# Sample attention in visits of three cache tiles, tokens stored by parity, in a one-core decoder layer

## The chip, the cores and the metric

The kernel is one program on one core of a Trainium2 chip. The metric is the device time of one execution in microseconds (us); the time of a kernel is the median of its runs. The profile and the trace describe one further execution. In them PE is TensorE's matmul stream, PEld its weight loads, DVE is VectorE, ACT is ScalarE, POOL is GpSimd, and SP is the engine whose queue issues nearly all DMAs.

## What is computed

One decoder layer for 256 prompt tokens and 8 x 4 = 32 sample tokens together (288 columns, D = 2048, all in float32). Cut to what matters:

```python
z = x @ w_in                      # h, Bg, Cg, q, k, v, g_a, g_b
ya = Bg * causal_conv3(Cg * h)
# q, k, v: 3 groups (dilation 1, 4, 16) x 4 heads of 128; token t sees t - dil*i, i = 0..128
yb = attention(q, k, v)           # softmax over all groups of a head together
mixed = sigmoid(g_a) * (ya @ w_branch_a) + sigmoid(g_b) * (yb @ w_branch_b)
x1 = LN1(ALPHA * x + mixed @ w_out)
a, b = split(x1 @ w_up);  a = causal_conv3(a)
y = LN2(ALPHA * x1 + (silu(a) * b) @ w_down)
```

The prompt attends to itself only; the sample tokens also attend to a cache of old keys and values. The windows of cache rows, the last rows of both convolutions and the new keys and values are outputs too.

## The kernel before

**The products.** All weights stream once from HBM in blocks of 128 output features, up to 1 MB each. `prepare` (L162) issues a block's load on SP into one of three `wst` buffers, and `half_block` (L135) splits it, half by half, into a rounded part `whi` (ACT, L138) and the rest `wlo` (DVE, L139). `product` (L187) then runs `mms` (L202): per 128 input features three fp32r matmuls of 288 columns (L208 hi x hi, L209 hi x lo, L210 lo x hi), 48 for a full block, 36 for a block of the last third of the FFN. The activations are split likewise (`split`, L213). A token tensor is read as two halves of 144 tokens, one column from each in turn; the layer's input `xh`, `xl` lies with a pitch of HX = 160 elements between the halves, all others with 144. So the two columns of a pair in PSUM belong to tokens t and t + 144.

**The order of the products.** 12 blocks for q, 24 for k and v, 48 for the convolution mixer, 32 for gate a and `w_branch_a`, 32 for gate b and `w_branch_b`, 16 for `w_out` with LayerNorm 1 (class `Norm`, L614), then three parts of the FFN: `w_up` blocks and 16 `w_down` blocks each. The program is written in that order, and a scheduler of the framework orders each engine's instructions by dependences and its own estimate of time; `behind` and `in_a_row` add ordering edges by hand.

**Prompt attention** (L320) of head j begins when its k and v are there, and is cut by `yield` into three pieces which `prompt_step` puts behind later products: the scores (L326: for query blocks 0 and 1 of 128 tokens, 3 groups each, against 128 or 256 keys; 1152 columns of plain f32 matmuls), the softmax (DVE, ACT), then transposes of v (L346) and of the weights (L354: 9), and the weighted sums (L362: 9 matmuls of 128 columns). Distances and masks lie in `m_dist`.

**Sample attention** (`sample_steps`, L406) goes through the 18 tiles (1 MB) of cached keys, does a softmax, and goes through the 18 tiles of cached values. A *visit* takes the tiles in SBUF, two of them (two buffers `cache`): for each batch 4 matmuls, one per head, each in its own 32 columns of the PE array, with queries (or weights) that a mask has put to zero outside the batch (`by_batch`, L379, one DVE product of 1024 columns per group). L421 are the key visits, L474 the value visits, 9 of each. After a visit `fetch_two` (L389) issues two loads (L395) and the two stores of the tiles into the output windows (L396), all on SP. Visits are spread evenly from the first k block on: each product adds 20 to a count and each 101 of it call for a step. L438 holds the scores of the new keys, L485 the share of the new values, as matmul groups of their own.

**Elsewhere.** `gated` (L555), `conv_in`, `pieces` and `from_psum` move between halves and token order in three instructions per tensor. In the last FFN part POOL subtracts the mean estimate from each chunk of `dd` (L785) and adds up sums for LayerNorm 2 (L639, L640). The tail (`finish_out`, L673) normalises and stores y.

Of the kernel before, what the change touches and what calls it, by code (L numbers as in the profile page):

```python
# [17 lines left out]
P = 128  # L18
D = 2048
KD = D // P  # L20
SEQ = 256
# [4 lines left out]

H = T // 2
HG = H + 1
HX = 160
# [13 lines left out]
SW = NG * P + NG * NS  # L43
SLOPE = [[float(np.float32(2.0 ** (-8.0 * (g * NH + j + 1) / (NG * NH)))) for j in range(NH)] for g in range(NG)]
# [6 lines left out]
C_M0 = C_TM + NT  # L51
C_M1 = C_M0 + NG * P
# [16 lines left out]


N_STEP = N_CT + 2
N_STEP_BLOCKS = 2 * NG * NH + 5 * KD - 3
# [11 lines left out]
def layer_kernel(ctx: ExitStack, tc: tile.TileContext, ins, outs):  # L84
# [25 lines left out]

    def att(cols=512):
        return sb(ps, [P, cols], "att", bufs=2)
# [8 lines left out]
    spent = [0]  # L121
# [12 lines left out]

    def half_block(st, k0, n):  # L135
        hi = sb(wp, [P, HK, P], "whi", F32R, bufs=4)
        lo = sb(wp, [P, HK, P], "wlo", F32R, bufs=4)
        act.copy(hi[:, :n, :], st[:, k0 : k0 + n, :])  # L138
        dve.tensor_tensor(lo[:, :n, :], st[:, k0 : k0 + n, :], f32(hi[:, :n, :]), ALU.subtract)  # L139
        return hi, lo, n  # L140
# [46 lines left out]
    def product(x):  # L187

        w = w_ready.pop(0)
        if not w_ready:  # L190
            prepare()
        if steps_on[0]:
            spent[0] += N_STEP
            while spent[0] >= N_STEP_BLOCKS:
                spent[0] -= N_STEP_BLOCKS
                next(steps, None)
        o = acc(x[0].shape[-1])
        mms(o, w, x)
        prompt_step()
        return o.rearrange("p a h -> p h a")  # L200
# [36 lines left out]
    w_two_lo = [sb(wk, [P, 2, HK, P], "cache", F32R, bufs=2) for _ in range(2)]  # L237
# [46 lines left out]
    cst = sb(big, [P, C_M0], "cst")  # L284

    pa = sb(big, [P, KD * T], "yal")
    m_dist = pa[:, : C_W - C_M0]
    pa_at = [C_W - C_M0]

# [5 lines left out]
    s_two = [pa_take(NG * 2 * P) for _ in range(2)]  # L295
    xs_flat = xs.rearrange("p k t -> p (k t)")
    q_all = xs_flat[:, : NH * NG * T].rearrange("p (j g t) -> p j g t", j=NH, g=NG)
    sT_flat = [xs_flat[:, NH * NG * T + c * NG * P : NH * NG * T + (c + 1) * NG * P] for c in range(3)]
    sT_three = [t.rearrange("p (g q) -> p g q", g=NG) for t in sT_flat]
# [14 lines left out]

    def in_a_row(row):

        for before, i in zip(row, row[1:]):
            behind(i, before)

    def prompt_attention(j, qT, kT, vT):  # L320

        blocks = [(qb, g, P * (qb + 1)) for qb in range(2) for g in range(NG)]
        s3 = att(NG * P), att(2 * 2 * P), sb(ps, [P, 2 * P], "acc")
        p_at = [(s3[0], g * P) for g in range(NG)] + [(s3[1], 0), (s3[1], 2 * P), (s3[2], 0)]
        in_a_row([last_mm[0]] + [
            pe.matmul(t[:, c : c + nk], qT[:, g, qb * P : (qb + 1) * P], kT[:, g, :nk], start=True, stop=True)  # L326
            for (t, c), (qb, g, nk) in zip(p_at, blocks)
        ])
        s = [s_two[qb][:, : NG * P * (qb + 1)].rearrange("p (g k) -> p g k", g=NG) for qb in range(2)]
        for (t, c), (qb, g, nk) in zip(p_at, blocks):  # L330
            c0 = qb * NG * P + g * nk
            dve.scalar_tensor_tensor(
                s[qb][:, g, :], m_dist[:, c0 : c0 + nk], -SLOPE[g][j] / SCALE, t[:, c : c + nk], ALU.mult, ALU.add
            )
        for qb in range(2):
            st = sb(wk, [P, 4], "st", bufs=4)
            dve.reduce_max(st[:, 0:1], s[qb], AX.XY)
# [8 lines left out]
            pe.transpose(pv[kb][:, g * P : (g + 1) * P], vT[:, g, kb * P : (kb + 1) * P], ident)  # L346
# [4 lines left out]
        pairs = ((0, 0), (1, 0), (1, 1))  # L351
        pt = [att(NG * P), att(NG * P), sb(ps, [P, NG * P], "acc")]
        in_a_row(row + [
            pe.transpose(t[:, g * P : (g + 1) * P], s[qb][:, g, kb * P : (kb + 1) * P], ident)  # L354
            for t, (qb, kb) in zip(pt, pairs) for g in range(NG)
        ])
        for sT, t in zip(sT_three, pt):
            act.copy(sT, t.rearrange("p (g q) -> p g q", g=NG))
# [4 lines left out]
                po[:, qb * P : (qb + 1) * P], v[:, kb, g], sT[:, g],  # L363
                start=kb == 0 and g == 0, stop=kb == qb and g == NG - 1,
            )
            for sT, (qb, kb) in zip(sT_three, pairs) for g in range(NG)
        ])
        act.copy(oT, po)
        split(ybh[:, j, :SEQ], ybl[:, j, :SEQ], oT)


    bmask = cst[:, C_BM : C_BM + NB * NS].rearrange("p (b r) -> p b r", b=NB)
    tmask = cst[:, C_TM : C_TM + NT]

    sw = sb(wk, [P, NH * NB * NS + 1152], "sw", bufs=1)
    sw_m = sw[:, : NH * NB * NS].rearrange("p (j b r) -> p j b r", j=NH, b=NB)
    sw2 = sw[:, NH * NB * NS :]

    def by_batch(src):  # L379

        m = sw_m
        shape = [P, NH, NB, NS]
        dve.tensor_tensor(m, src.unsqueeze(2).broadcast_to(shape), bmask.unsqueeze(1).broadcast_to(shape), ALU.mult)
        return m
# [21 lines left out]
    def sample_steps():  # L406
        fetch_two()
        yield
        row = []
        s = sw2[:, :SW]  # L410
        sbias = cst[:, C_SB : C_SB + SW]
        for g in range(NG):
            qm = by_batch(q_s[:, g])
            cols = P if g == 0 else NT * P
            p = sb(ps, [P, cols], "long", bufs=1)
            for b in range(NB):
                if g > 0 or b % 4 == 0:
                    c = cache_tiles.pop(0)
                o = (b % 4) * NH * P if g == 0 else 0
                for j in range(NH):  # L420
                    row.append(pe.matmul(  # L421
                        p[j * NS : (j + 1) * NS], qm[:, j, b, :], c[:, o + j * cols : o + (j + 1) * cols],
                        start=b == 0, stop=b == NB - 1,
                    ))
                if b == NB - 1 or (g > 0 and b % 2 == 1):
                    in_a_row(row)
                    row = []
                    fetch_two()
                    yield
# [5 lines left out]
        pn = sb(ps, [P, NG * NS], "long", bufs=1)  # L435
        for j in range(NH):
            for g in range(NG):
                pe.matmul(  # L438
                    pn[j * NS : (j + 1) * NS, g * NS : (g + 1) * NS], q_s[:, g, j, :], k_s[:, g, j, :],
                    start=True, stop=True,  # L440
                )
        dve.tensor_tensor(s[:, NG * P :], pn, sbias[:, NG * P :], ALU.add)
        st = sb(wk, [P, 4], "st", bufs=4)
        dve.reduce_max(st[:, 0:1], s, AX.X)
        dve.tensor_scalar_mul(st[:, 1:2], st[:, 0:1], -SCALE)
        act.activation(s, s, AF.Exp, bias=st[:, 1:2], scale=SCALE, accum_out=st[:, 2:3])
        dve.reciprocal(st[:, 3:4], st[:, 2:3])
        dve.tensor_scalar_mul(s, s, st[:, 3:4])
        pt = att()
        for g in range(NG):  # L450
            pe.transpose(pt[:, g * P : (g + 1) * P], s[:, g * P : (g + 1) * P], ident)
        pt2 = att()
        pe.transpose(pt2[: NG * NS, :P], s[:, NG * P :], ident)
        sT = sw2[:, : NG * P].rearrange("p (g r) -> p g r", g=NG)
        act.copy(sT, pt[:, : NG * P].rearrange("p (g r) -> p g r", g=NG))
        sTn = sw2[: NG * NS, NG * P : NG * P + P]
        act.copy(sTn, pt2[: NG * NS, :P])
        vn = sw2[: NG * NS, NG * P + P : NG * P + P + NH * P].rearrange("p (j d) -> p j d", j=NH)
        pv = att()
        for j in range(NH):  # L460
            pe.transpose(pv[: NG * NS, j * P : (j + 1) * P], v_s[:, j].rearrange("p g r -> p (g r)"), ident)
        act.copy(vn, pv[: NG * NS].rearrange("p (j d) -> p j d", j=NH))
        o_sb = sw2[:, NG * P + P + NH * P : NG * P + 2 * P + NH * P]
        for g in range(NG):
            sm = by_batch(sT[:, g].rearrange("p (j r) -> p j r", j=NH))
            cols = P if g == 0 else NT * P
            if g < 2:
                p = sb(ps, [P, cols], "long", bufs=1)
            for b in range(NB):
                if g > 0 or b % 4 == 0:  # L470
                    c = cache_tiles.pop(0)
                o = (b % 4) * NH * P if g == 0 else 0
                for j in range(NH):
                    row.append(pe.matmul(  # L474
# [502 lines left out]
```

## Time and profile before

| | |
|---|---|
| median of 3 runs | 1762.09 us (1761.49 to 1762.12) |
| the profiled execution | 1763.11 us, span 1761.3 us |
| granted TensorE clock, mean | 0.997 of full speed |
| busy share: PE, DVE, ACT, POOL | 99%, 57%, 45%, 14% |
| HBM traffic over the span | 275 GB/s |

The span is the part of an execution that the trace covers; the profiled execution was 1.8 us longer than its span and 1.0 us longer than the median. A busy PE need not be PE at its peak: the time between the starts of two matmuls tells the pace.

### The profile page before, as it was taken

The numbers are of one execution on the slowest core, as the hardware profiler recorded it, in microseconds if no ns is written. First come the engines' busy times: TensorE is split into PE (matmuls) and PEld (weight loads), VectorE is DVE, ScalarE is ACT, GpSimd is POOL, SyncE is SP. The second block draws the span as 40 slices with busy tenths as digits, with TensorE's granted clock in tenths as the row PEclk, the third lists the DMA queues.
The fourth block names the chain that finished last, engine by engine and source line by source line (L and its number), as shares of the span: only waits on it lengthen the run. The fifth ranks groups of instructions, "written<-read, shape, count | busy, mean of one in ns | idle before, by whom it ended". The sixth has DMA issues, their size and how long they took to land.

```text
span 1761.3 us, 33600 instructions
## 1 busy us (share of the span) xinstructions
PE 1743.9 (99%) x14269; PEld 1714.4 (97%) x14269; DVE 1008.2 (57%) x1322; ACT 798.4 (45%) x1174; POOL 254.8 (14%) x403
## 2 busy tenths in 40 slices
PE   9999999999999999999999999999999999999996
PEld 9999999999999999999999999999999999999996
DVE  5444455545555444455588888774555554555554
ACT  5444444333434333344445656553454443345444
POOL 0000000000000000001155233310011110011174
PEclk9999999999999999999999999999999999999998
DMA  8477787787787887466766566656565656666662
GB/s 325 173 288 264 271 299 297 265 324 297 271 333 285 304 312 269 150 241 252 269 259 220 210 241 226 229 219 236 219 236 219 236 217 238 217 238 217 223 212 105
DMA packets 60919, 436.25 MB, mean 248 GB/s; under 512 B 7265, under 2 KB 8929, under 8 KB 16865
## 3 DMA queue, kind: packets, MB, share of 16 engines
q1 hardware_dynamic: 59040, 429.40, 65.9%
q10 hardware_dynamic: 1728, 4.72, 0.7%
q8 instruction: 111, 1.82, 0.4%
q14 instruction: 40, 0.32, 0.0%
HBM read 389.89 MB, written 94.53 MB: 275 GB/s over the span
## 4 chain that ended last, share of the span: by engine, by line
PE 96%; POOL 1%; ACT 1%; DVE 1%; issue 0%; DMA 0%; ACTq 0%; DVEq 0%
PE acc L208 31%; PE acc L210 31%; PE acc L209 31%; PE acc L276 1%; PE long L421 1%; PE long L474 1%; POOL dd L785 1%; PE att L362 0%; PE att L326 0%; ACT whi L138 0%; POOL qk_s L549 0%; ACT xh L214 0%; ACT yah L708 0%; DVE dd L684 0%; DMA yah<-in_x 0%
## 5 line engine op out<-in xcount | busy, mean ns | idle before, releaser
L139 DVE TENSOR_TENSOR wlo<-wst,whi 128x1024 fp32r<-128x1024 f32 (+1 forms) x578 | 706.9, 1224 | 617.3 <-ACT whi L138 613.2
L138 ACT CAST whi<-wst 128x1024 fp32r<-128x1024 f32 (+1 forms) x578 | 590.0, 1022 | 871.2 <-PE acc L209 767.7
L208 PE MATMUL acc<-xh,whi 128*128 128x288 f32 (+1 forms) x3216 | 923.0, 287 | 0.0
L210 PE MATMUL acc<-xh,wlo 128*128 128x288 f32 (+1 forms) x3216 | 920.5, 286 | 0.0
L209 PE MATMUL acc<-xl,whi 128*128 128x288 f32 (+1 forms) x3216 | 920.4, 286 | 0.0
L208 PEld LDWEIGHTS acc<-xh,whi 128*128 128x128 f32 x3216 | 607.8, 189 | 7.9 <-ACT h L569 2.5
L210 PEld LDWEIGHTS acc<-xh,wlo 128*128 128x128 f32 x3216 | 607.8, 189 | 0.8 <-issue 0.8
L209 PEld LDWEIGHTS acc<-xl,whi 128*128 128x128 f32 x3216 | 607.9, 189 | 0.3 <-issue 0.2
L208 PE MATMUL acc<-yah,whi 128*128 128x288 f32 x1216 | 348.0, 286 | 0.3 <-ACT yah L214 0.3
L210 PE MATMUL acc<-yah,wlo 128*128 128x288 f32 x1216 | 347.7, 286 | 0.6 <-DVE wlo L139 0.6
L209 PE MATMUL acc<-yal,whi 128*128 128x288 f32 x1216 | 347.6, 286 | 0.0
L208 PEld LDWEIGHTS acc<-yah,whi 128*128 128x128 f32 x1216 | 229.7, 189 | 3.1 <-ACT h L591 2.5
L210 PEld LDWEIGHTS acc<-yah,wlo 128*128 128x128 f32 x1216 | 229.8, 189 | 0.8 <-DVE wlo L139 0.8
L209 PEld LDWEIGHTS acc<-yal,whi 128*128 128x128 f32 x1216 | 229.8, 189 | 0.0
L549 POOL COPY qk_s<-u 128x2 f32<-128x2 f32 x44 | 41.5, 943 | 565.7 <-ACT u L758 441.1
L535 DVE SCALAR_TENSOR_TENSOR cy<-u,prm,cy 128x304 f32<-128x304 f32 x120 | 71.1, 593 | 3.4 <-ACT cy L533 0.7
L606 POOL TENSOR_TENSOR ya<-ya,dd 128x288 f32<-128x288 f32 x16 | 13.6, 851 | 306.0 <-DVE ya L605 306.0
L560 DVE TENSOR_TENSOR ya<-cy,acc 128x144 f32<-128x144 f32 x132 | 25.6, 250 | 33.6 <-PE acc L210 33.6
L549 POOL COPY cm<-u 128x2 f32<-128x2 f32 x16 | 3.0, 185 | 254.3 <-DVE u L574 254.3
L214 ACT CAST yah<-ya 128x288 fp32r<-128x288 f32 x76 | 32.7, 430 | 13.8 <-POOL ya L606 8.3
L214 DVE TENSOR_TENSOR yal<-ya,yah 128x288 fp32r<-128x288 f32 x76 | 34.9, 460 | 1.3 <-ACT yah L214 1.2
L639 POOL TENSOR_TENSOR cache<-cache,dd 128x288 f32<-128x288 f32 x29 | 28.0, 964 | 49.0 <-DVE dd L724 33.5
(179 smaller groups left out, 852.8 us busy)
## 6 DMA issues: line engine op xcount, KB each, us to landing
wst<-in_w_in SPq DMA_DIRECT2D x113, 1024.0 KB, 6.0
wst<-in_w_up SPq DMA_DIRECT2D x88, 1024.0 KB, 4.8
wst<-in_w_down SPq DMA_DIRECT2D x32, 1024.0 KB, 4.8
cache<-in_ck SPq DMA_DIRECT2D x18, 1024.0 KB, 6.4
out_o_ck<-cache SPq DMA_DIRECT2D x18, 1024.0 KB, 9.1
cache<-in_cv SPq DMA_DIRECT2D x18, 1024.0 KB, 6.3
out_o_cv<-cache SPq DMA_DIRECT2D x18, 1024.0 KB, 9.8
wst<-in_w_a SPq DMA_DIRECT2D x16, 1024.0 KB, 4.8
```

What stands on the lines that cost most here:

```text
L138: act.copy(hi[:, :n, :], st[:, k0 : k0 + n, :])
L139: dve.tensor_tensor(lo[:, :n, :], st[:, k0 : k0 + n, :], f32(hi[:, :n, :]), ALU.subtract)
L208: pe.matmul(out, hi[:, c, :], xh_k, start=k == 0, stop=False)
L209: pe.matmul(out, hi[:, c, :], xl_k, start=False, stop=False)
L210: last_mm[0] = pe.matmul(out, lo[:, c, :], xh_k, start=False, stop=k == nk - 1)
L214: return act.copy(hi, src), dve.tensor_tensor(lo, src, f32(hi), ALU.subtract)
L276: i = pe.matmul(o[b], first_w(term == 2, b, k), xk, start=k == 0 and term == 0, stop=k == KD - 1 and term == 2)
L421: row.append(pe.matmul(p[j * NS : (j + 1) * NS], qm[:, j, b, :], c[:, o + j * cols : o + (j + 1) * cols], start=b == 0, stop=b == NB - 1,))
L535: dve.scalar_tensor_tensor(y, u[:, i : i + YW], prm[:, w0 + i : w0 + i + 1], y, ALU.mult, ALU.add)
L549: pool.tensor_copy(dst[:, 0:2], u[:, SEQ : SEQ + 2])
L560: dve.tensor_tensor(a, b, c, ALU.mult)
L639: pool.tensor_tensor(self.s1, self.s1, d, ALU.add)
```

## The change

1. **Tokens by parity.** The two halves of a token tensor now hold the even and the odd tokens, so that a pair of PSUM columns is a pair of neighbours. `split` of the input reads x with a step of two; `conv_in`'s callers and `gated` write and read token order with a step of two, in two instructions where there were three (in part 0 of the FFN `gated` takes three where it took two). HX falls from 160 to 145.
2. **Prompt attention.** The query blocks are the even and the odd tokens. Dilations 4 and 16 keep the parity, so groups 1 and 2 need 128 keys per block and only group 0 needs 256: 1024 columns of score matmuls per head, 8 transposes of weights, 8 weighted sums.
3. **Sample attention.** Three `cache` buffers, and visits of three tiles, one each 8 products from the eighth q block on: 6 for keys and 6 for values. Each product calls `fetch`, which issues one load or one store. `by_batch` is called per batch, two products ahead of the visit. The new keys' scores and the new values' share ride in a visit. Accumulators lie partly in `att` buffers. Scratch moves into the `dd` buffer, and the mask array shrinks.
4. **Order.** Ordering edges put the re-split of x behind the splits of gated activations and weights (after part 0), and each subtraction of the mean on POOL behind the sums of three chunks earlier (last part).

The core of the diff:

```diff
-HX = 160
+HX = 145
+MW = (2 + NG - 1) * P
+N_VISIT = 3
+APART = 8
...
     def product(x):
         if steps_on[0]:
-            spent[0] += N_STEP
-            while spent[0] >= N_STEP_BLOCKS:
-                spent[0] -= N_STEP_BLOCKS
-                next(steps, None)
+            next(steps, None)
...
-        splits.append(split(xh[:, k, :, :H], xl[:, k, :, :H], h3(xs[:, k])))
+        splits.append(split(xh[:, k, :, :H], xl[:, k, :, :H], xs[:, k].rearrange("p k (a h) -> p k h a", h=2)))
...
     def prompt_attention(j, qT, kT, vT):
+        q4 = h3(qT)[:, :, :, :P]
+        k4, v4 = (t[:, :, :SEQ].rearrange("p g (a h) -> p g h a", h=2) for t in (kT, vT))
+        for qb in range(2):
+            row += [
+                pe.matmul(s3[qb][:, : 2 * P], q4[:, 0, qb], kT[:, 0, :SEQ], start=True, stop=True)
+            ] + [
+                pe.matmul(s3[qb][:, (1 + g) * P : (2 + g) * P], q4[:, g, qb], k4[:, g, qb], start=True, stop=True)
+                for g in range(1, NG)
+            ]
...
-    def fetch_two():
-        for _ in range(2):
+    def fetch():
+        if to_store:
+            sp.dma_start(*to_store.pop())
+        elif len(cache_tiles) < N_VISIT:
             which, n = next(cache_left, (None, 0))
             if which:
-                t = sb(wk, [P, 2048], "cache", bufs=2)
+                t = sb(wk, [P, 2048], "cache", bufs=3)
                 behind(sp.dma_start(t, ins[which][n]), w_load[0])
-                sp.dma_start(outs["o_" + which][n], t)
+                to_store.append((outs["o_" + which][n], t))
                 cache_tiles.append(t)
...
+        for values in range(2):
+            p = [None] * NG
+            for first in range(0, N_CT, N_VISIT):
+                here = held[first : first + N_VISIT]
+                for n in range(APART):
+                    fetch()
+                    if values and first == 0 and n == 3:
+                        transposed()
+                    if n == APART - 2:
+                        at = 0
+                        for g, batches in here:
+                            for b in batches:
+                                by_batch(at, sT[:, g].rearrange(...) if values else q_s[:, g], b)
+                                at += 1
+                    yield
...
+                        for j in range(NH):
+                            row.append(pe.matmul(
+                                p[g][j * NS : (j + 1) * NS], sw_m[:, len(row) // NH, j], c[:, o + j * cols : o + (j + 1) * cols],
...
+                if values and 0 in rest_of:
+                    row += [ ... the share of the new values, into p[0] ... ]
+                elif not values and NG - 1 in rest_of:
+                    pn = att(NG * NS)
+                    row += [ ... the scores of the new keys, into pn ... ]
+                in_a_row(row)
...
         for i in range(KD):
             o = product((h3(gh), h3(gl)))
             if part == 0:
-                split(x[0][:, i], x[1][:, i], h2(dd[:, i]))
+                for i_x, *before in zip(split(x[0][:, i], x[1][:, i], h2(dd[:, i])), last_split, w_split):
+                    for b in before:
+                        behind(i_x, b)
...
                 if f == KF and i > 0:
-                    pool.tensor_tensor(dd[:, i], dd[:, i], n2.c, ALU.subtract)
+                    i_c = pool.tensor_tensor(dd[:, i], dd[:, i], n2.c, ALU.subtract)
+                    if i > 2:
+                        behind(i_c, sums[i - 3])
```

More of the change, by code (lines that the diff above doesn't have):

```diff
@@ L137, in half_block @@
         lo = sb(wp, [P, HK, P], "wlo", F32R, bufs=4)
-        act.copy(hi[:, :n, :], st[:, k0 : k0 + n, :])
-        dve.tensor_tensor(lo[:, :n, :], st[:, k0 : k0 + n, :], f32(hi[:, :n, :]), ALU.subtract)
+        w_split[:] = split(hi[:, :n, :], lo[:, :n, :], st[:, k0 : k0 + n, :])
         return hi, lo, n
@@ L236, in layer_kernel @@
     w_two_hi = sb(big, [P, 2, KD, P], "yal", F32R)
-    w_two_lo = [sb(wk, [P, 2, HK, P], "cache", F32R, bufs=2) for _ in range(2)]
+    w_two_lo = [sb(wk, [P, 2, HK, P], "cache", F32R, bufs=3) for _ in range(2)]
     w_in_two = ins["w_in"][0:2].rearrange("b p (k c) -> p b k c", c=P)
@@ L313, in layer_kernel, with load_distances @@
     v_s = sb(big, [P, NH, NG, NS], "v_s")
+    def load_distances():
+        pool.memset(m_dist[: P // 2, :, :, P:], BIG)
+        m0, m1 = (
+            ins["cst"][:, c : c + NG * n * P].rearrange("(a h) (g k) -> h a g k", h=2, g=NG)
+            for n, c in ((1, C_M0), (2, C_M1))
+        )
+        for h in range(2):
+            behind(sp.dma_start(m_dist[: P // 2, h, :, :P], m0[h]), w_load[0])
+            behind(sp.dma_start(m_dist[P // 2 :, h], m1[h]), w_load[0])
     def in_a_row(row):
@@ L320, in prompt_attention @@
     def prompt_attention(j, qT, kT, vT):
[L322 to L334, printed above, removed]
+        q4 = h3(qT)[:, :, :, :P]
+        k4, v4 = (t[:, :, :SEQ].rearrange("p g (a h) -> p g h a", h=2) for t in (kT, vT))
+        s3 = [att(MW) for _ in range(2)]
+        row = [last_mm[0]]
+        for qb in range(2):
[6 more added lines that the diff above has]
+        in_a_row(row)
+        s = s_two
+        for qb in range(2):
+            for g in range(NG):
+                c, n = (0, 2 * P) if g == 0 else ((1 + g) * P, P)
+                m = m_dist[:, qb, g] if g == 0 else t2(m_dist[:, qb, g])[:, qb]
+                dve.scalar_tensor_tensor(
+                    s[qb][:, c : c + n], m, -SLOPE[g][j] / SCALE, s3[qb][:, c : c + n], ALU.mult, ALU.add
+                )
         for qb in range(2):
             st = sb(wk, [P, 4], "st", bufs=4)
-            dve.reduce_max(st[:, 0:1], s[qb], AX.XY)
+            dve.reduce_max(st[:, 0:1], s[qb], AX.X)
             dve.tensor_scalar_mul(st[:, 1:2], st[:, 0:1], -SCALE)
@@ L350, in prompt_attention @@
             act.copy(v[:, kb], pv[kb].rearrange("p (g d) -> p g d", g=NG))
-        pairs = ((0, 0), (1, 0), (1, 1))
-        pt = [att(NG * P), att(NG * P), sb(ps, [P, NG * P], "acc")]
+        pt = [sb(ps, [P, MW], "acc") for _ in range(2)]
         in_a_row(row + [
-            pe.transpose(t[:, g * P : (g + 1) * P], s[qb][:, g, kb * P : (kb + 1) * P], ident)
-            for t, (qb, kb) in zip(pt, pairs) for g in range(NG)
-        ])
-        for sT, t in zip(sT_three, pt):
-            act.copy(sT, t.rearrange("p (g q) -> p g q", g=NG))
+            pe.transpose(pt[qb][:, c * P : (c + 1) * P], s[qb][:, c * P : (c + 1) * P], ident)
+            for qb in range(2) for c in range(MW // P)
+        ])
+        for sT, t in zip(sT_two, pt):
+            act.copy(sT, t)
         yield 1
@@ L362, in prompt_attention, with by_batch @@
             pe.matmul(
-                po[:, qb * P : (qb + 1) * P], v[:, kb, g], sT[:, g],
-                start=kb == 0 and g == 0, stop=kb == qb and g == NG - 1,
+                po[:, qb * P : (qb + 1) * P], v[:, c if c < 2 else qb, max(0, c - 1)], sT_two[qb][:, c * P : (c + 1) * P],
+                start=c == 0, stop=c == MW // P - 1,
             )
-            for sT, (qb, kb) in zip(sT_three, pairs) for g in range(NG)
+            for qb in range(2) for c in range(MW // P)
         ])
         act.copy(oT, po)
[L369 to L384, printed above, removed]
+        split(h2(ybh[:, j])[:, :, :P], h2(ybl[:, j])[:, :, :P], oT.rearrange("p (h a) -> p h a", h=2))
+    bmask = cst[:, C_BM : C_BM + MASK]
+    tmask = cst[:, C_BM + MASK :]
+    sw_m = sb(wk, [P, 2 * NH + 1, NH, NS], "sw", bufs=1)
+    dd_all = sb(big, [P, KD * T], "dd")
+    kv = dd_all[:, : 2 * 2 * NG * T].rearrange("p (b c g t) -> p b c g t", b=2, c=2, g=NG)
+    sw2 = dd_all[:, 2 * 2 * NG * T :]
+    def by_batch(n, src, b):
+        m = bmask[:, (NB - 1 - b) * NT : (NB - 1 - b) * NT + NS]
+        dve.tensor_tensor(sw_m[:, n], src, m.unsqueeze(1).broadcast_to([P, NH, NS]), ALU.mult)
     cache_left = iter([(which, n) for which in ("ck", "cv") for n in range(N_CT)])
     cache_tiles = []
-    def fetch_two():
-        for _ in range(2):
+    to_store = []
+    def fetch():
+        if to_store:
+            sp.dma_start(*to_store.pop())
+        elif len(cache_tiles) < N_VISIT:
             which, n = next(cache_left, (None, 0))
             if which:
-                t = sb(wk, [P, 2048], "cache", bufs=2)
+                t = sb(wk, [P, 2048], "cache", bufs=3)
                 behind(sp.dma_start(t, ins[which][n]), w_load[0])
-                sp.dma_start(outs["o_" + which][n], t)
+                to_store.append((outs["o_" + which][n], t))
                 cache_tiles.append(t)
@@ L406, in sample_steps, with scored @@
     def sample_steps():
-        fetch_two()
-        yield
-        row = []
         s = sw2[:, :SW]
         sbias = cst[:, C_SB : C_SB + SW]
[L412 to L429, printed above, removed]
+        sT = sw2[:, : NG * P].rearrange("p (g r) -> p g r", g=NG)
+        sTn = sw2[: NG * NS, NG * P : NG * P + P]
+        vn = sw2[: NG * NS, NG * P + P : NG * P + P + NH * P].rearrange("p (j d) -> p j d", j=NH)
+        o_sb = sw2[:, NG * P + P + NH * P : NG * P + 2 * P + NH * P]
+        held = [(0, range(4)), (0, range(4, NB))] + [(g, (b,)) for g in range(1, NG) for b in range(NB)]
+        def scored(g, p):
             sg = s[:, g * P : (g + 1) * P]
@@ L434, in sample_steps @@
                 pick_t(sg, p, sbias[:, g * P : (g + 1) * P])
[L435 to L470, printed above, removed]
-                    c = cache_tiles.pop(0)
-                o = (b % 4) * NH * P if g == 0 else 0
-                for j in range(NH):
-                    row.append(pe.matmul(
-                        p[j * NS : (j + 1) * NS], sm[:, j, b, :], c[:, o + j * cols : o + (j + 1) * cols],
-                        start=b == 0 and g < 2, stop=b == NB - 1 and g == 2,
-                    ))
-                if b == NB - 1 or (g > 0 and b % 2 == 1):
-                    in_a_row(row)
-                    row = []
-                    fetch_two()
-                    yield
-            if g == 0:
-                for j in range(NH):
-                    pe.matmul(
-                        p[j * NS : (j + 1) * NS], sTn[:, j * NS : (j + 1) * NS], vn[:, j, :], start=False, stop=True
-                    )
-                act.copy(o_sb, p)
-            elif g == 2:
-                pick_t(o_sb, p, o_sb)
@@ new lines, in softmax, with transposed @@
+        def softmax():
+            dve.tensor_tensor(s[:, NG * P :], pn, sbias[:, NG * P :], ALU.add)
+            st = sb(wk, [P, 4], "st", bufs=4)
+            dve.reduce_max(st[:, 0:1], s, AX.X)
+            dve.tensor_scalar_mul(st[:, 1:2], st[:, 0:1], -SCALE)
+            act.activation(s, s, AF.Exp, bias=st[:, 1:2], scale=SCALE, accum_out=st[:, 2:3])
+            dve.reciprocal(st[:, 3:4], st[:, 2:3])
+            dve.tensor_scalar_mul(s, s, st[:, 3:4])
+        def transposed():
+            pt, pt2 = att(), att()
+            row = [pe.transpose(pt[:, g * P : (g + 1) * P], s[:, g * P : (g + 1) * P], ident) for g in range(NG)]
+            row.append(pe.transpose(pt2[: NG * NS, :P], s[:, NG * P :], ident))
+            act.copy(sT, pt[:, : NG * P].rearrange("p (g r) -> p g r", g=NG))
+            act.copy(sTn, pt2[: NG * NS, :P])
+            pv = att()
+            for j in range(NH):
+                row.append(pe.transpose(pv[: NG * NS, j * P : (j + 1) * P], v_s[:, j].rearrange("p g r -> p (g r)"), ident))
+            in_a_row(row)
+            act.copy(vn, pv[: NG * NS].rearrange("p (j d) -> p j d", j=NH))
@@ new lines, in sample_steps @@
+        for values in range(2):
[10 more added lines that the diff above has]
+                            for b in batches:
+                                by_batch(at, sT[:, g].rearrange("p (j r) -> p j r", j=NH) if values else q_s[:, g], b)
+                                at += 1
+                    yield
+                row = []
+                for g, batches in here:
+                    c = cache_tiles.pop(0)
+                    cols = P if g == 0 else NT * P
+                    for b in batches:
+                        if b == 0:
+                            p[g] = p[1] if values and g == 2 else att(P) if g == 0 else (
+                                att() if g == 2 else sb(ps, [P, cols], "long", bufs=1))
+                        o = (b % 4) * NH * P if g == 0 else 0
+                        for j in range(NH):
+                            row.append(pe.matmul(
+                                p[g][j * NS : (j + 1) * NS], sw_m[:, len(row) // NH, j], c[:, o + j * cols : o + (j + 1) * cols],
+                                start=b == 0 and not (values and g == 2), stop=b == NB - 1 and not (values and g < 2),
+                            ))
+                rest_of = [g for g, batches in here if NB - 1 in batches]
+                if values and 0 in rest_of:
+                    row += [
+                        pe.matmul(
+                            p[0][j * NS : (j + 1) * NS], sTn[:, j * NS : (j + 1) * NS], vn[:, j, :], start=False, stop=True
+                        )
+                        for j in range(NH)
+                    ]
+                elif not values and NG - 1 in rest_of:
+                    pn = att(NG * NS)
+                    row += [
+                        pe.matmul(
+                            pn[j * NS : (j + 1) * NS, k * NS : (k + 1) * NS], q_s[:, k, j, :], k_s[:, k, j, :],
+                            start=True, stop=True,
+                        )
+                        for k in range(NG) for j in range(NH)
+                    ]
+                in_a_row(row)
+                for g in rest_of:
+                    if not values:
+                        scored(g, p[g])
+                    elif g == 0:
+                        act.copy(o_sb, p[0])
+                    elif g == NG - 1:
+                        pick_t(o_sb, p[g], o_sb)
+            if not values:
+                softmax()
@@ L505, in layer_kernel @@
             act.copy(h2(q_all[:, j, g]), q_first.pop(0) if q_first else product(x))
-            if j == 1:
-                dst, src = ((cst, ins["cst"][:, :C_M0]), (m_dist, ins["cst"][:, C_M0:]), (prm, ins["prm"]))[g]
-                behind(sp.dma_start(dst, src), w_load[0])
-        pool.tensor_copy(q_s[:, :, j, :], q_all[:, j, :, SEQ:])
-    steps_on[0] = True
+            if j == 1 and g == 1:
+                load_distances()
+            elif j == 1:
+                for dst, src in ((prm, ins["prm"]),) if g else (
+                    (cst[:, :C_BM], ins["cst"][:, :C_BM]),
+                    (cst[:, C_BM : C_BM + MASK], ins["cst"][:, C_MASK : C_MASK + MASK]),
+                    (cst[:, C_BM + MASK :], ins["cst"][:, C_TM:C_M0]),
+                ):
+                    behind(sp.dma_start(dst, src), w_load[0])
+            steps_on[0] = j * NG + g >= NH * NG - 2 - APART // 2
+        pool.tensor_copy(q_s[:, :, j, :].rearrange("p g (a h) -> p g h a", h=2), h3(q_all[:, j])[:, :, :, P:])
     for j in range(NH):
@@ L557, in gated @@
         yt = y[:, SEQ : SEQ + NB * (NT + 2)].rearrange("p (b r) -> p b r", b=NB)
-        if add is None:
-            for a, b, c in zip(pieces(out, samples(out)), pieces(y, yt[:, :, 2:]), from_psum(o)):
+        for a, b, c in zip(of_halves(h2(out)), of_tokens(y[:, :SEQ], yt[:, :, 2:]), of_halves(o)):
+            if add is None:
                 dve.tensor_tensor(a, b, c, ALU.mult)
-        else:
-            for a, b, c in ((out[:, :SEQ], y[:, :SEQ], o[:, :SEQ]), (samples(out), yt[:, :, 2:], samples(o))):
+            elif len(a.shape) == 3:
                 dve.scalar_tensor_tensor(a, c, add, b, ALU.add, ALU.mult)
+            else:
+                for h in range(2):
+                    dve.scalar_tensor_tensor(a[:, h], c[:, h], add, b[:, h], ALU.add, ALU.mult)
     cm = sb(big, [P, KD, 2 + 2 * NB], "cm")
@@ L744, in layer_kernel @@
     n2 = Norm(R_LN + 2 * KD, R_LN + 3 * KD, True)
+    sums = []
     for part, nf in enumerate(THIRDS):
```

71 lines of the change are left out of this document (37 added, 34 removed).

## The prediction

> **What bounds the kernel now.** I read first the busy shares on the page, then who PE waited for, then PE's own timeline around everything that is not a product.
>
> ```profile
> span 1761.3 us, 33600 instructions
> ## 1 busy us (share of the span) xinstructions
> PE 1743.9 (99%) x14269; PEld 1714.4 (97%) x14269; DVE 1008.2 (57%) x1322; ACT 798.4 (45%) x1174; POOL 254.8 (14%) x403
> ```
>
> PE has work nearly all the time. The waits of PE, all of them, as total, count and longest:
>
> ```profile
> PE acc L226 <- DVE cy L223: 1.2, 1, 1.2
> PE acc L210 <- DVE wlo L139: 0.6, 1, 0.6
> PE acc L208 <- ACT yah L214: 0.3, 1, 0.3
> PE acc L276 <- ACT yal L214: 0.2, 1, 0.2
> ```
>
> Four waits, 2.3 us; two of them (1.2 and 0.2) belong to the start. So no DMA and no other engine holds PE up anywhere in the attention stages: what counts there is how long PE's own instructions take. Off PE the change can win next to nothing; it can only lose, by making a new wait. The pace of the products, from a stretch that holds nothing else (busy us and matmuls of PE come first):
>
> ```profile
> 26.50:114.00 87.50, 87.50 (x717) 87.50 (x716) 38.92 (x34) 36.11 (x49) 5.05 (x7) 1.00 0.66 248
> ```
>
> 87.50 / 717 = 0.122 us per matmul. What an insertion costs PE is then the time from the start of the last product matmul before it to the start of the second one after it, less 2 x 0.122.
>
> **Part 1: the visits.** Three insertions from PE's timeline (start, length, what): an ordinary visit of two tiles, the value visit with 64 short records, and the small group of 8 records at L485.
>
> ```profile
> 251.63 1.92 PE L421 MATMUL long<-cache,sw 128*32 128x512 f32 x16
> ...
> 456.16 0.29 PE L208 MATMUL acc<-xh,whi 128*128 128x288 f32 x1
> 456.37 1.95 PE L474 MATMUL long<-cache,sw 128*32 128x128 f32 x64
> ...
> 458.48 0.29 PE L210 MATMUL acc<-xh,wlo 128*128 128x288 f32 x1
> ...
> 476.86 0.29 PE L210 MATMUL acc<-xh,wlo 128*128 128x288 f32 x1
> 477.07 0.43 PE L485 MATMUL long<-sw 96*32 96x128 f32 x8
> ...
> 477.66 0.29 PE L209 MATMUL acc<-xl,whi 128*128 128x288 f32 x1
> ```
>
> The first lasts as long as the second, 1.92 and 1.95 us: 16 records are four times as wide and stand for 64. The other two cost 458.48 - 456.16 - 0.24 = 2.08 and 477.66 - 476.86 - 0.24 = 0.56 us with 64 and 8 records of one kind: (2.08 - 0.56) / 56 = 0.027 per record, which leaves 0.56 - 8 x 0.027 = 0.34 us that does not depend on the number. So each time PE goes over to these narrow matmuls and back it loses some 0.34 us, and a tile costs 32 x 0.027 = 0.87. The work of the 36 tiles stays. What goes are the changes of mode: before there are 18 visits, one of them broken in two by transposes (the row at 131.30 below), L438 and L485, 21 in all; the order of the changed program has 12 blocks, with L438's and L485's matmuls inside two of them. 9 x 0.34 = **3.1 us** less. A visit of three tiles should cost as much as 96 short records, 96 x 0.027 + 0.34 = 2.9.
>
> **Part 2: prompt attention.** The rows show the broken visit, the weighted sums of one head, and its 9 transposes of weights:
>
> ```profile
> 131.30 0.42 PE L421 MATMUL long<-cache,sw 128*32 128x128 f32 x6
> ...
> 138.24 2.17 PE L362 MATMUL att<-yah,yal 128*128 128x128 f32 x18
> 140.17 0.37 PE L208 MATMUL acc<-xh,whi 128*128 128x288 f32 x1
> ...
> 174.22 0.87 PE L354 MATMUL att<-cst,yal 128*128 128x128 f32 x6
> 174.93 0.49 PE L354 MATMUL acc<-cst,yal 128*128 128x128 f32 x3
> 175.18 0.37 PE L208 MATMUL acc<-xh,whi 128*128 128x288 f32 x1
> ```
>
> 9 matmuls of 128 columns (18 records) take 140.17 - 138.24 = 1.93, so 0.214 each; 9 transposes 175.18 - 174.22 = 0.96, so 0.107 each. Per head the scores lose 1152 - 1024 = 128 columns (0.214), the transposes one of 9 (0.107), the sums one of 9 (0.214): 0.535, for 4 heads **2.1 us** less. DVE and ACT lose as many elements of the softmax, which no PE wait depends on.
>
> **Part 3: the two late waits.** The chain that ended last shows how the 0.6 us at L210 came about:
>
> ```profile
> 1688.44 9.40 POOL dd L785 x8
> ...
> 1700.42 0.81 POOL cache L640
> ...
> 1702.67 1.91 DVE wlo L139
> ```
>
> All of POOL's subtractions (L785) stood in one row, the sums (L640) behind them; ACT's squares need the buffers that the sums read, ACT's `whi` casts stand behind the squares, and so a `wlo` came late. In the changed order one subtraction stands between the sums of each chunk. The 0.3 us at L208 came from re-splits of x standing ahead of the split of a gated activation; they now stand behind it. I count both as gone, **0.9 us**. If the new edges did nothing, both would stay, and the 0.9 would be lost to the sum.
>
> **What is added, and costed at nothing.** (a) *More DVE instructions*: 48 masks of 128 columns for 6 of 1024, fewer and longer instructions in `conv_in` and `gated`. DVE is busy 57% of the span and the split weights stand ready ahead of PE, as the list of waits shows; a visit with 9 masks gives DVE at most 9 x 0.46 us (the 288 columns of the row below) two products (48 x 0.122 = 5.9 us each) ahead. (b) *Accesses with a step of two floats.* Nearest rows, a DVE sum with a step of two in PSUM and one with none:
>
> ```profile
> L214 DVE TENSOR_TENSOR yal<-ya,yah 128x288 fp32r<-128x288 f32 x76 | 34.9, 460 | 1.3 <-ACT yah L214 1.2
> ...
> L786 DVE TENSOR_TENSOR dd<-dd,acc 128x288 f32<-128x288 f32 x32 | 14.4, 450 | 18.8 <-PE acc L210 18.8
> ```
>
> 450 against 460 ns: no price. In SBUF no row shows it; if such an instruction took twice its 0.46 us, the path would feel it only at the first split and in some 6 instructions of the tail, under 3 us. None can be faster than one without a step, so the other end is 0. I take 0. (c) *Strided operands on PE* in 16 score matmuls and 16 transposes: at twice their 0.214 and 0.107 us 5 us, at the least 0; I take 0, as PE already reads pairs from two far halves at full pace. (d) *The pitch of 145.* The pitch is 160 in the first of these rows and 144 in the second:
>
> ```profile
> L209 PE MATMUL acc<-xl,whi 128*128 128x288 f32 x2704 | 773.4, 286 | 0.0
> L208 PE MATMUL acc<-yah,whi 128*128 128x288 f32 x1216 | 348.0, 286 | 0.3 <-ACT yah L214 0.3
> ```
>
> 286 ns both; I take no change. An odd pitch is not in the trace, so the first rival is about it. (e) *SP's queue.* A load or store stands between two weight loads where two loads and two stores stood together. A load behind a visit still waits for PE, and the weight loads queued behind it with it, as before; three weight buffers hide it now, and if they did not, PE would show waits for L139.
>
> **The sum.** 3.1 + 2.1 + 0.9 = 6.1 us. The profiled execution's span of 1761.3 would become 1755.2, that execution 1763.1 - 6.1 = 1757.0; it stood 1.0 above the median of the runs, from which I count: 1762.1 - 6.1 = **1756.0**. A measurement of this kernel can tell some 0.2%, 3.5 us, from no change: faster means below 1758.6, slower above 1765.6.
>
> **The rivals.**
>
> *The pitch slows PE (the other side).* Place: every matmul on x, three for each of 2704 and 512 input chunks (L208 to L210), 9648. Price: 1 ns on each is 9.6 us. From 0.64 ns the gain is gone, from 1.0 ns the kernel is slower by over 0.2%; at 2 ns it would take 1756.0 + 19.3 = 1775. For it: 145 floats is an odd pitch, the two columns of a pair lie differently to any alignment. Against: 144 and 160 give the same 286 ns, and so no alignment effect is seen so far.
>
> *The visits wait.* Accumulators in `att` are shared with prompt attention, masks come per batch, the third tile is loaded late. If each of 12 visits waited once as long as the two late waits above, 0.3 to 0.6 us, 3.6 to 7.2 come back: 1759.6 to 1763.2. For it: visits now also carry the small groups, which need more to be ready. Against: tiles arrive a visit ahead, and the order puts no prompt piece between the allocation of an accumulator and its release that needs the same buffer.
>
> *POOL and DVE block each other in the last part.* Stretches of it, DVE fourth and POOL eighth in each row as busy us:
>
> ```profile
> 1686.00:1698.00 12.00, 12.00 (x101) 12.00 (x100) 7.93 (x9) 4.63 (x7) 12.00 (x11) 1.00 0.75 273
> 1705.00:1742.00 37.00, 37.00 (x305) 37.00 (x304) 20.46 (x26) 18.20 (x27) 21.50 (x22) 1.00 0.38 129
> ```
>
> Here a product takes 36 x 0.122 = 4.4 us. In the second stretch POOL does 21.50 / 11 = 1.95 us per product and DVE 20.46 x 4.4 / 37 = 2.43, of which 0.45 reads PSUM; the first adds 12.00 / 11 = 1.1 per product on POOL. If the two excluded each other, 1.95 + 1.1 + 1.98 = 5.0 us, 0.6 more than the product, in 13 products 8 us: 1764. But in the first stretch POOL was busy for 12.00 of 12 us and DVE for 7.93 all the same, so they do not. The Trainium skill says under "SBUF: two separate sides" of the page "SBUF — State Buffer" that an instruction of VectorE with two SBUF inputs and one of GpSimd that reads SBUF exclude each other for the whole instruction; by that rule this rival would be the forecast, and the trace does not agree with it.
>
> *The change does not do what it says*: the changed order shows the 12 blocks, so I give it nothing.
>
> **How the numbers follow.** Forecast 70%: 1756.0, and for itself 1753.5 to 1758.5 (the 0.9 or the 0.34 a little off). Waiting visits 14%, POOL and DVE 4%: both within 0.2%. Pitch or another access 12%: slower. That gives faster 0.70, same 0.18, slower 0.12. The range takes in the forecast, the waiting visits and the prices of (b) and (c), 1756 + 3 + 5: 1753.0 to 1764.0, which leaves out some 0.15.
>
> **What would show it.** Right: 12 groups of narrow matmuls of 2.9 us each; 16 records in place of 18 in a head's sums, 0.2 us shorter; L785 single on POOL; no PE wait after 30 us of over 0.1; 286 ns on the rows of x. Wrong: a mean above 287 ns there (pitch); PE waits for `cache`, `sw` or `att` ahead of visits; PE waits for `wlo` (SP's queue or DVE late); a tail longer than 17 us from the last product matmul.

## The result and the profile after

| | before | changed |
|---|---|---|
| median | 1761.66 us (14 runs, 1761.42 to 1762.37) | 1757.92 us (14 runs, 1757.47 to 1758.60) |
| ratio | | 0.9978, 95% interval 0.9972 to 0.9985 |
| last product matmul starts (traces) | 1744.05 us; 1742.88 in a second trace | 1738.55 us |

The kernel became 3.7 us faster where 6.1 were forecast. The page of the changed kernel, and all waits of its PE:

```profile
span 1756.1 us, 33532 instructions
## 1 busy us (share of the span) xinstructions
PE 1738.7 (99%) x14257; PEld 1713.2 (98%) x14257; DVE 1009.0 (57%) x1320; ACT 797.8 (45%) x1142; POOL 244.8 (14%) x404
```

```profile
PE acc L234 <- DVE cy L231: 1.2, 1, 1.2
PE acc L284 <- ACT yal L222: 0.6, 1, 0.6
PE acc L284 <- ACT whi L222: 0.3, 1, 0.3
```

The two late waits are gone, and the three that are left belong to the first 10 us: no visit waits for a tile, a mask or an accumulator. Now a visit of three tiles and one head's weighted sums, from PE's timeline (start, length, what):

```profile
467.89 0.28 PE L218 MATMUL acc<-xh,wlo 128*128 128x288 f32 x1
468.10 2.78 PE L501 MATMUL long<-cache,sw 128*32 128x512 f32 x24
...
471.04 0.29 PE L217 MATMUL acc<-xl,whi 128*128 128x288 f32 x1
```

```profile
137.44 1.95 PE L390 MATMUL att<-yah,yal 128*128 128x128 f32 x16
139.14 0.37 PE L216 MATMUL acc<-xh,whi 128*128 128x288 f32 x1
```

The visit costs 471.04 - 467.89 - 0.24 = 2.91 us (forecast 2.9), the sums 1.70 us in place of 1.93. Reckoned like this, all insertions between the products from the fourth on take 62.86 us in the trace of before and 57.63 in that of the changed kernel: 5.23 us, just what parts 1 and 2 of the prediction come to. So the attention gave all that was forecast, and something else took back some. PE's pace shows it. The first rows are the first and the last of the 720 product matmuls before the first insertion in the kernel before, the second rows those of the 576 in the changed kernel:

```profile
26.28 0.29 PE L208 MATMUL acc<-xh,whi 128*128 128x288 f32 x1
...
114.36 0.29 PE L210 MATMUL acc<-xh,wlo 128*128 128x288 f32 x1
```

```profile
25.09 0.28 PE L216 MATMUL acc<-xh,whi 128*128 128x288 f32 x1
...
95.68 0.28 PE L218 MATMUL acc<-xh,wlo 128*128 128x288 f32 x1
```

88.08 / 719 = 0.12250 us from start to start before, 70.59 / 575 = 0.12277 after: 0.27 ns more on each matmul that reads x. Over the whole trace the products that read x run at 122.50 ns from start to start before and 122.78 after (some 8,100 matmuls of 288 columns), those that read other tensors at 122.5 in both. 8,100 x 0.28 ns = 2.3 us. The 1,536 matmuls on x of the second gate read 290 columns; they went from 123.33 to 123.47 ns, another 0.2 us.

### The profile page after: what moved, and what is told of

Same layout as the page of the kernel before. It is cut to its first block, busy times and chain, and to the rows that moved or that the text cites. A ratio compares the mean times of both kernels' runs of the same rounds, so it can differ in the third digit from the quotient of the medians.

```text
span 1756.1 us, 33532 instructions
## 1 busy us (share of the span) xinstructions
PE 1738.7 (99%) x14257; PEld 1713.2 (98%) x14257; DVE 1009.0 (57%) x1320; ACT 797.8 (45%) x1142; POOL 244.8 (14%) x404
## 4 chain that ended last, share of the span: by engine, by line
PE 99%; DMA 0%; DVE 0%; ACT 0%; SPq 0%; ACTq 0%; issue 0%; DVEq 0%
PE acc L216 32%; PE acc L218 31%; PE acc L217 31%; PE long L501 1%; PE acc L284 1%; PE att L501 1%; PE att L390 0%; DMA wst<-in_w_in 0%; ACT yah L759 0%; DVE dd L735 0%; PE att L350 0%; PE acc L382 0%; PE att L348 0%; PE att L373 0%; PE att L699 0%; PE att L698 0%
## 5 line engine op out<-in xcount | busy, mean ns | idle before, releaser
L222 DVE TENSOR_TENSOR wlo<-wst,whi 128x1024 fp32r<-128x1024 f32 (+2 forms) x584 | 709.8, 1216 | 600.9 <-ACT whi L222 596.9
L222 ACT CAST whi<-wst 128x1024 fp32r<-128x1024 f32 (+2 forms) x584 | 593.2, 1016 | 888.5 <-PE acc L217 785.0
L596 POOL COPY qk_s<-u 128x2 f32<-128x2 f32 x44 | 37.9, 862 | 572.6 <-ACT u L810 449.6
L607 DVE TENSOR_TENSOR ya<-cy,acc 128x256 f32<-128x256 f32 x88 | 23.4, 307 | 34.8 <-PE acc L218 34.8
```

Source lines behind the costliest of these rows:

```text
L222: return act.copy(hi, src), dve.tensor_tensor(lo, src, f32(hi), ALU.subtract)
L596: pool.tensor_copy(dst[:, 0:2], u[:, SEQ : SEQ + 2])
L607: dve.tensor_tensor(a, b, c, ALU.mult)
```

## Experiments

**Theory**: the pitch of 145 between the halves of x costs PE 0.27 ns per matmul, and what counts is that it is odd; the attention gives 5.2 us; the ordering edges give the rest. **Rivals**: the slower pace is the run's or comes from other accesses; another property of the pitch counts; the gain of the visits lies in the spread of loads and stores, not in their number.

**The pitch alone, in the kernel before** (`b_hx145`):

```diff
-HX = 160
+HX = 145
```

> The kernel before with HX = 145 in place of 160, nothing else. Theory (pitch): each matmul on x takes 0.26 ns longer, as the starts of PE's matmuls show in the changed kernel (122.72 against 122.46 ns over 8,000 of them), so some 2.2 us more than before, ratio 1.0012, and the pace of the x products in the trace is 122.7 ns. Rival (the missing 2.4 us lie elsewhere, in strided accesses or new waits): ratio 1.0000 and a pace of 122.5 ns.

Measured 1763.86 us, ratio 1.0011 (1.0003 to 1.002), and the pace of the same 720 matmuls:

```profile
25.46 0.28 PE L208 MATMUL acc<-xh,whi 128*128 128x288 f32 x1
...
113.74 0.28 PE L210 MATMUL acc<-xh,wlo 128*128 128x288 f32 x1
```

88.28 / 719 = 0.12278. One number of the layout, with nothing else changed, brings the slower pace; the median is 1.65 us above that of the kernel before in the same series (1762.21), with 0.5 to 3.5 us as the interval, and in its trace the way from the fourth product to the last is 2.3 us longer than in that of before. The rival that the slower pace is the run's or comes from other accesses falls.

**Other pitches**: the kernel before with 146 and 147 (`b_hx146`, `b_hx147`), the changed kernel with 146 and 148 (`a_hx146`, `a_hx148`), each by one line as above. For 148 the changed kernel needs space, so one array of constants goes as well:

```diff
-    ones_p = sb(big, [P, P], "ones_p", F32R)
...
-            pe.matmul(p, ones_p, hi, start=True, stop=True)
-            act.copy(self.c, p)
+            pe.matmul(p, ones_d, hi, start=True, stop=True)
+            act.activation(self.c, p, AF.Copy, scale=float(KD))
```

> The kernel before with HX = 146, even. If an odd pitch costs: 122.45 ns, as with 160. If what counts is how close the two halves lie: 122.7 ns, as with 145.

> The kernel before with HX = 147, odd again (588 bytes). If an odd pitch costs: x products at 122.7 ns per matmul, as with 145. If 145 alone does (for being one more than the number of columns read, say): 122.5 ns.

> The changed kernel with HX = 146, an even pitch (584 bytes). If the odd pitch is what costs: x products back at 122.5 ns, 2.2 us less than the changed kernel, 1755.7 us, ratio 0.9966. If the pitch must be a multiple of 16 bytes or more: still 122.7 ns and ratio 0.9978. If the pitch has nothing to do with it: 0.9978 with 122.7 ns whatever the pitch.

> The changed kernel with HX = 148 (592 bytes, a multiple of 16); the space comes from one constant array, whose one use takes the other constant array and a factor of 16 in the copy behind it. If oddness or multiples of up to 16 bytes decide: 122.5 ns and 1755.7 us, ratio 0.9966, 4.2 us below the kernel before plus the 1.9 that the pitch takes back. If only multiples of 64 bytes are free: 122.7 ns and 0.9978.

First and last of the 720 matmuls with 146 and with 147, then of the 576 in the changed kernel with 146 and with 148:

```profile
25.49 0.29 PE L208 MATMUL acc<-xh,whi 128*128 128x288 f32 x1
...
113.57 0.29 PE L210 MATMUL acc<-xh,wlo 128*128 128x288 f32 x1
```

```profile
25.24 0.29 PE L208 MATMUL acc<-xh,whi 128*128 128x288 f32 x1
...
113.52 0.28 PE L210 MATMUL acc<-xh,wlo 128*128 128x288 f32 x1
```

```profile
24.75 0.29 PE L216 MATMUL acc<-xh,whi 128*128 128x288 f32 x1
...
95.19 0.29 PE L218 MATMUL acc<-xh,wlo 128*128 128x288 f32 x1
```

```profile
25.52 0.29 PE L216 MATMUL acc<-xh,whi 128*128 128x288 f32 x1
...
95.95 0.29 PE L218 MATMUL acc<-xh,wlo 128*128 128x288 f32 x1
```

88.08 / 719 = 0.12250 with 146, 88.28 / 719 = 0.12278 with 147, and 70.44 / 575 = 0.12250 and 70.43 / 575 = 0.12249 in the changed kernel with 146 and 148. Both odd pitches cost the same, and 144 (the pitch of the other tensors), 146, 148 and 160 run at the same pace of 122.5 ns. So neither how near the halves lie nor being a multiple of more than two floats matters among these. That it is oddness rests on two odd and four even pitches. Single runs of the kernel before took 1762.36 us (146) and 1764.38 (147). The changed kernel takes **1755.29 us** with 146 (ratio 0.9963, 0.9951 to 0.9976) and 1755.74 with 148 (0.9965, 0.9952 to 0.9979): both beat the changed kernel by over 2 us, and the version with 146 differs from it in one digit.

**Two tiles per visit** (`a_visit2`):

```diff
-N_VISIT = 3
-APART = 8
+N_VISIT = 2
+APART = 5
```

> The changed kernel with two tiles per visit, one visit each 5 products: 18 visits for 12, all else as changed. Theory (each change of mode costs PE 0.34 us whatever the visit holds): 6 x 0.34 = 2.0 us more than the changed kernel, 1759.9 us, ratio 0.9990, visits of 2.06 us each. Rival (the gain of the visits lies in the single loads and stores between them, or in the work per tile): ratio 0.9978.

Measured 1759.70 us, ratio 0.9988 (0.9979 to 0.9997), 1.8 us more than the changed kernel. One of its visits:

```profile
521.01 0.28 PE L218 MATMUL acc<-xh,wlo 128*128 128x288 f32 x1
521.22 1.92 PE L501 MATMUL long<-cache,sw 128*32 128x512 f32 x16
...
523.30 0.29 PE L217 MATMUL acc<-xl,whi 128*128 128x288 f32 x1
```

523.30 - 521.01 - 0.24 = 2.05 us. All insertions together take 59.63 us, 2.00 more than in the changed kernel, which has six visits fewer: 0.33 us for each. Loads and stores go one by one here too, and the tiles are the same 36, so the number of visits is what counts. Matmuls that use the whole array show no such fixed price when they are put in between products: 9 of the weighted sums cost 1.93 us and 8 cost 1.70, in proportion to their number to within 0.02 us.

**Without the ordering edges** (`a_noedges`):

```diff
-                for i_x, *before in zip(split(x[0][:, i], x[1][:, i], h2(dd[:, i])), last_split, w_split):
-                    for b in before:
-                        behind(i_x, b)
+                split(x[0][:, i], x[1][:, i], h2(dd[:, i]))
...
-                    if i > 2:
-                        behind(i_c, sums[i - 3])
```

> The changed kernel without the ordering edges of its fourth part (re-split of x, subtraction of the mean on POOL). Theory (part 3): the two late waits of the kernel before come back, PE shows 0.6 us behind wlo near 1700 us and some 0.3 us behind the split of a gated activation near 1160 us, with the restart after them 0.9 to 1.3 us; 1758.8 to 1759.2 us, ratio 0.9983 to 0.9986. Rival (the waits went with the shorter token-order instructions, not with the edges): no such waits, 1757.9 us, ratio 0.9978.

Measured 1759.39 us, ratio 0.9987 (0.9978 to 0.9997); the last product matmul starts at 1740.01 us in its trace, 1.46 later than with the edges. Two of its PE waits, and the chain ahead of the first:

```profile
PE acc L218 <- DVE wlo L222: 0.6, 1, 0.6
...
PE acc L216 <- ACT yah L222: 0.4, 1, 0.4
```

```profile
1684.38 9.40 POOL dd L837 x8
...
1698.61 1.93 DVE wlo L222
1700.59 0.39 PE acc L218
```

Both waits are back where they were. So the edges removed them, not the shorter instructions around.

**The kernel before once more** (`b_again`):

> The kernel before, unchanged, for a second trace. The trace of before ran its first 13 matmuls of weights at half pace and reached the fourth product at 26.28 us, that of the changed kernel at 25.09. If this is the run's luck with the clock and not the kernel's: the first product matmul lies anywhere between 24.7 and 26.3 us, and the run's time moves with it. If it is the kernel's: 26.3 again. Theory for the rest: 122.46 ns on x, the 0.6 and 0.3 us waits as before.

```profile
25.05 0.29 PE L208 MATMUL acc<-xh,whi 128*128 128x288 f32 x1
```

The fourth product began 1.2 us earlier than in the first trace of the same program (26.28), whose first matmuls on weights ran at half pace (0.24 us apart until 10.7 us), and the run took 1761.96 us, not 1763.11. So that part of the 5.5 us between the two traces' last product matmuls is the run's luck; why that start was slow is open, as the granted clock reads 1.00 there in both traces. Against this second trace the changed kernel is 1742.88 - 1738.55 = 4.33 us ahead there.

## Why the prediction was nearly right

*Part 1, the visits (3.1 us) and part 2, prompt attention (2.1 us)*: right in mechanism and size, 5.2 us by the trace. `a_visit2` shows the price per visit. Part 2 is read from traces alone; no run isolates it.

*Part 3, the two late waits (0.9 us)*: right that the edges remove them, too small, and one step of the first wait was missed. The list of waits counts from the end of one matmul's record to the next start. A record is 0.29 us long where the starts are 0.12 apart, and the second start behind a wait comes 0.23 us after the first. In the kernel before:

```profile
1702.67 1.90 DVE L139 TENSOR_TENSOR wlo<-wst,whi 128x1024 fp32r<-128x1024 f32 x1 [5.48 <-ACT whi L138]
1702.69 0.80 POOL L639 TENSOR_TENSOR cache<-cache,dd 128x288 f32<-128x288 f32 x1
...
1703.74 0.29 PE L209 MATMUL acc<-yal,whi 128*128 128x288 f32 x1
1704.62 0.39 PE L210 MATMUL acc<-yah,wlo 128*128 128x288 f32 x1 [0.60 <-DVE wlo L139]
1704.85 0.29 PE L208 MATMUL acc<-yah,whi 128*128 128x288 f32 x1
```

1704.85 - 1703.74 - 0.24 = 0.87 us by the starts, of which 0.60 stood in the list. `a_noedges` measured 1.5 us for both waits. The missed step is in the first two rows: this `wlo` takes 1.90 us where others take 1.22. As shown below under *POOL and DVE*, it was held up by the sum of LayerNorm 2 that POOL ran at the same time. Without these 0.68 us the matmul at 1704.62 could have started at 1703.94, and at the undisturbed pace it was due at 1703.86. So nearly all of this wait needed both the late `whi` and POOL. This is an estimate from the rows; no run separates the two.

*(d), the pitch: "286 ns both; I take no change".* This is the step that failed. 160 and 144 are both even, so the rows said nothing about an odd pitch, and the column that was read cannot show it:

```profile
L217 PE MATMUL acc<-xl,whi 128*128 128x288 f32 x2704 | 773.1, 286 | 0.0
```

This is the changed kernel, at the slower pace, and its mean is again 286 ns. The records of these matmuls overlap: each is 286 ns long and the next starts 122.5 ns after it, so the length does not tell the pace; the distance of the starts does. The sign "a mean above 287 ns" was blind to the effect that it was to reveal. The mechanism stood among the rivals, at 1 or 2 ns per matmul; it was 0.27, too little to use up the gain. With it the sum closes: 5.2 + 1.5 - 2.3 - 0.2 = 4.2 us, against 4.33 in the traces and 3.7 in the medians. Some 0.3 us more are lost behind the last product matmul: the span ends 17.6 us after it in every trace with the tokens by parity and 17.3 in every other. Counted from there, the last store of y lands 0.1 us later; why another 0.2 follow is open. The rest is within the spread of the runs. That the forecast of 1756.0 missed by only 1.9 us is in part luck: part 3 was 0.6 too small, and so hid some of the 2.5 that the pitch took.

*(a), (c), (e)*: right. PE waits for none of it, and for (c) the scores of a head cost 1.97 us with 1152 columns before and 1.77 with 1024 after, 1.7 ns a column in both. *(b)*: right for DVE, a little off for ACT. ACT's first split of x, 576 elements, with a step of one before and of two after:

```profile
L214 ACT CAST xh<-yah 128x576 fp32r<-128x576 f32 x4 | 2.7, 669 | 0.9 <-DMA yah<-in_x 0.9
```

```profile
L222 ACT CAST xh<-yah 128x576 fp32r<-128x576 f32 x4 | 2.9, 730 | 1.2 <-DMA yah<-in_x 1.2
```

*POOL and DVE*: the rival did not come, but the reason given against it was wrong. The changed kernel's timeline in the last part:

```profile
1689.86 0.80 POOL L839 TENSOR_TENSOR dd<-dd,cache 128x288 f32<-128x288 f32 x1
1689.89 1.85 DVE L222 TENSOR_TENSOR wlo<-wst,whi 128x1024 fp32r<-128x1024 f32 x1 [1.40 <-ACT whi L222]
...
1698.32 0.79 POOL L839 TENSOR_TENSOR dd<-dd,cache 128x288 f32<-128x288 f32 x1
1698.72 1.47 DVE L222 TENSOR_TENSOR wlo<-wst,whi 128x1024 fp32r<-128x1024 f32 x1 [1.78 <-ACT whi L222]
```

Elsewhere this `wlo` takes 1.22 us. It starts 0.77 us before POOL's subtraction ends and takes 0.63 longer, or 0.39 us before and takes 0.25 longer: it waits for POOL, with some 0.14 us of its own in the shadow. The whole trace bears this out. The 437 such `wlo` that overlap no work of POOL take 1.21 to 1.23 us; the 47 that start while a sum, product or subtraction of POOL has over 0.2 us left all take longer by what is left less 0.14 us, to within 0.01. In the other order POOL waits: one of its instructions of 0.80 us that starts just behind a `wlo` lasts 1.78. The trace of before shows the same, in 46 cases, so the prediction could have read it. POOL and DVE busy for 12.00 and 7.93 us of 12 do not disprove an exclusion, since blocked time counts as busy. (In the prediction's rows POOL's busy time is the sixth figure, not the eighth.) The trace does agree with the rule that the prediction cited from "SBUF: two separate sides" of the Trainium skill's page "SBUF — State Buffer".

Why PE does not wait all the same can be estimated from the sum without blocked time: three POOL instructions at 0.80 and 1.22 + 0.68 on DVE make 4.3 us, just inside the 4.4 us of a product. No run tests this.

## What to carry to other kernels

Where PE never waits, count what it does between its products, and the price of going over to matmuls in a part of the array with it: fewer and larger visits pay that price less often. When a layout constant changes, read the pace from the starts of the first and the last of some hundred matmuls, not from their lengths: 0.2% on most matmuls (2.5 us here) outweighs a well-made saving elsewhere (part 2, 2.1 us). Busy time does not show that two engines work side by side: compare an instruction's length with and without the other engine at work. A buffer that has to shrink by a few elements may have a neighbour size that costs nothing.

## What the runs showed of the hardware

- fp32r matmuls that read pairs of columns from two far halves of a tensor started 122.5 ns apart for 288 columns with a pitch of 144, 146, 148 and 160 floats, and 122.77 to 122.79 with 145 and 147. Why an odd pitch costs is open.
- Matmuls in 32 of 128 columns cost 0.33 to 0.34 us per change to them and back, whether 2 or 3 tiles follow, and 0.027 us per record of 128 columns.
- A subtraction with two inputs in SBUF on DVE (1.22 us) and one on POOL (0.80 us) did not run side by side: the later one was held up until the earlier one ended, less 0.14 us where DVE was the later.
- Reading SBUF with a step of two floats cost DVE nothing (754 ns on average for 576 elements of the first split of x in both kernels) and took ACT from 669 to 730 ns.
